# The 1/rms row of a norm, spread over the partitions by a trip through DRAM instead of by products with the identity

## The chip, the cores and the metric

The kernel runs on one core of a Trainium2 chip. What is measured is the device time of one execution in microseconds (us), as the median of several. Smaller is better.

A core has several engines that work side by side, each through its own list of instructions in order: TensorE (PE in the profile, with its weight loads as PEld), VectorE (DVE), ScalarE (ACT), GpSimd (POOL) and SyncE (SP), which in this kernel issues the transfers between DRAM and the on-chip memory SBUF. Where one needs what another makes, it waits on a semaphore, and everything queued behind it on that engine waits too.

## What is computed

A small decoder trunk on x of 1024 tokens by 1024 features: two layers, each a mixer and a SwiGLU feed-forward network (FFN), with a norm ahead of each and one at the end. Cut to what matters here:

```python
def rmsnorm(x, g):
    y = x * lax.rsqrt(jnp.mean(x * x, axis=-1, keepdims=True) + RMS_EPS)
    return y * g

def swiglu(h, w_gate, w_up, w_down):
    return (jax.nn.silu(h @ w_gate) * (h @ w_up)) @ w_down

def reference(x, ...):
    h = x
    for layer in range(2):
        hn = rmsnorm(h, mix_norm_g[layer])
        h = h + (even_mixer(hn, ...) if layer % 2 == 0 else odd_mixer(hn, ...))
        h = h + swiglu(rmsnorm(h, ffn_norm_g[layer]), ...)
    return rmsnorm(h, final_norm_g)
```

The even mixer holds a pooling mixer and a state-space scan (SSD), the odd one an RWKV-7 scan and a gated recurrence; each has an input and an output projection.

## The kernel before

**Layout.** Activations lie transposed in SBUF: features on the 128 partitions, tokens along the free axis. The 1024 tokens are worked on in two halves (hf 0 and 1) of H = 512; one tile is 128 features by 512 tokens, and eight tiles make a half. All large products run on TensorE in a split form: each operand is a high part and a low part, and three products (L370, L371, L372 in `dense`) make one. The weights come in blocks of 512 KB (`wload`, L323, issued on SP, three buffers `raw`), and are split by ACT (`whi`, L348) and DVE (`wlo`, L349) before TensorE uses them.

**Order.** `trunk` writes the stages of both halves one behind the other and weaves the scans in as side work: mixer and FFN of layer 0, half 0; output projection and then FFN of half 1, and so on. The order of instructions on each engine is not that of the text: the program is built under a context that schedules by a simulated time line, so a change in one place can move instructions around it.

**The norms.** `Stat.add` squares and sums the eight tiles of a half to one tile `nacc` (a token's sum is still spread over the partitions). `Stat.rstd` (L264 to L280) finishes it:

- L269: four products of TensorE with a column of ones sum `nacc` over the partitions. The result `ps_st` has 128 partitions by 4 columns: token c*128+p stands on partition p in column c.
- L272 and `rsqrt` (L206 to L215): twelve small DVE instructions on the tile `nst` make y = 1/rms in that form. The last of them is always an L215.
- L276: y is needed as a row r, along the free axis and the same on all partitions. Four products (y broadcast along the free axis, times the 128x128 identity) make it in `ps_rb`, eight PE instructions in the trace since a float32 product takes two passes.
- L279: ACT copies `ps_rb` to the SBUF tile `nrb` (128 by 512, two buffers). That is r.

`rstd` runs six times, mostly by `later(2, ...)`, that is two steps of `dense` behind the end of the sums. The numbers 1 to 6 are used below:

1. behind the output projection of half 0 in layer 0; r is used by the gate and up step of the FFN (DVE at L495, POOL at L498), whose input goes unscaled into the product (`gain_apply`), while the SSD of half 1 runs as side work;
2. behind that FFN; r is used by `norm_apply` (L300 on POOL, L304 on DVE) for the odd mixer of half 0;
3. behind the output projection of half 1; used by `norm_apply` for the FFN of half 1;
4. behind the FFN of half 1; used by `norm_apply` inside the output projection of half 0 in layer 1. Here the tiles are loaded back from DRAM (`hraw`, L285);
5. behind that output projection; used by `norm_apply` for the FFN of half 0 in layer 1;
6. behind the output projection of half 1 in layer 1; used by `stras_norm` (DVE at L598), which prepares the input of the last FFN. That FFN is computed by Strassen's scheme (products `py` at L663 and on, weights split by DVE and ACT); meanwhile the last steps of half 0's FFN run, with its final norm (`xo`, L583).

Elsewhere the kernel already spreads small values over the partitions through DRAM: the SSD's running sums (`cumT` to `cumd` at L901, loaded with a broadcast at L984) and the RWKV's norm of k (L1231 and L1262). The RWKV also copies a tile X to DRAM as `xd` in short runs and reads it back (L1352).

Of the kernel before, what the change touches and what calls it, by code (L numbers as in the profile page):

```python
# [5 lines left out]
F32 = mybir.dt.float32  # L6
# [7 lines left out]
P = 128  # L14
D = 1024
S = 1024
H = 512
# [69 lines left out]
class Trunk:  # L87
# [16 lines left out]
    def setup(self):  # L104
        nc, i = self.nc, self.i
        cst = self.cp.tile([P, NCONST], F32, name="cst")
        nc.gpsimd.dma_start(cst[:, :P], i["const"][:, :P])
        nc.gpsimd.dma_start(cst[:, P:], i["const"][:, P:NCONST])
        for n, (o, w) in CONST_COLS.items():
            if o < NCONST:  # L110
                setattr(self, "c_" + n, cst[:, o:o + w])
        self.ones = self.cp.tile([P, P], F32, name="ones")
        nc.gpsimd.memset(self.ones, 1.0)
        self.q = []


    def later(self, n, fn):
# [131 lines left out]
    class Stat:  # L249
# [15 lines left out]
        def rstd(self):  # L265
            tr, nc = self.tr, self.tr.nc
            ps = tr.psum("ps_st")
            for c in range(4):
                nc.tensor.matmul(ps[:, c:c + 1], self.acc[:, c * P:(c + 1) * P], tr.ones[:, :1], start=c == 0, stop=c == 3)  # L269
            st = tr.dp.tile([P, 3, 4], F32, name="nst", tag="nst", bufs=2)  # L270
            x, y, t = st[:, 0, :], st[:, 1, :], st[:, 2, :]
            nc.vector.tensor_scalar(x, ps[:, :4], 1.0 / D, EPS, op0=MULT, op1=ADD)  # L272
            tr.rsqrt(y, x, t)
            ps2 = tr.psum("ps_rb")
            for c in range(4):
                nc.tensor.matmul(ps2[:, c * P:(c + 1) * P], y[:, c:c + 1].to_broadcast([P, P]), tr.c_ident,  # L276
                                 start=True, stop=True)
            r = tr.dp.tile([P, H], F32, name="nrb", tag="nrb", bufs=2)
            nc.scalar.copy(r, ps2)  # L279
            return r  # L280

    def hload(self, hf, k):
# [1293 lines left out]
def trunk(tc, ins, out):  # L1576
    with ExitStack() as stack:
# [11 lines left out]
        with tc.tile_pool(name="ep", bufs=1) as ep:  # L1589
            t.setup()  # L1590
            hn, blk = t.start(ep, "xbc", 10)
            t.setup_params()
            t.even_open(ep)
            sA, sB = {}, {}
            side = Side(t.ssd(0, sA))
            m = t.in0(0, hn, sA, blk)
            weave(m, side, RATES["ssd0"], 10)
            xt = t.load_x(1, ep, "xbc", 10)
            hn = []
            hand(m, 8, t.norm_x(hn, xt), side, RATES["ssd0"])  # L1600
            t.zsync = side.finish
            weave(t.in0(1, hn, sB), side, RATES["ssd0"])
            side.finish()
            t.flush()
            side = Side(t.ssd(1, sB))
            hA, hn = [], []
            g = t.gain_apply(hn, hA, "ffn_norm_g", 0)
            st = hand(t.outproj(0, 0, wo0, t.yd[0], hA), 8, g, side, RATES["o0"], (4, 2))
            run_all(g)
            R["A"] = st.rstd()  # L1610
            side.step(RATES["b0"])
            st = weave(t.ffn(0, 0, hA, hn, None, lambda: R["A"]), side, RATES["ssd1"])
            side.finish()
            t.later(2, lambda: rstd("A", st))
            hB, hn = [], []
            stB = hand(t.outproj(1, 0, wo0, t.yd[1], hB), 8,
                       t.norm_apply(hn, None, lambda: R["A"], "mix_norm_g", 8, 0))
            t.flush()
        t.later(2, lambda: rstd("B", stB))
        with tc.tile_pool(name="op", bufs=1) as op, ExitStack() as late:  # L1620
            t.odd_open(op, late.enter_context(tc.tile_pool(name="oq", bufs=1)))
# [4 lines left out]
            st = weave(t.ffn(1, 0, hB, hn2), side, RATES["rw"])  # L1626
            side.finish()
            t.later(2, lambda: rstd("B", st))
            hA = []
            m = t.outproj(0, 1, wo1, t.yd[0], hA, t.hn2)  # L1630
# [51 lines left out]
```

## Time and profile before

| what | us |
|---|---|
| median of 3 runs (lowest to highest) | 2426.74 (2424.93 to 2427.56) |
| the profiled execution | 2427.69 |
| its span, first to last instruction | 2425.9 |
| TensorE busy | 2373.9 |
| VectorE busy | 1656.8 |
| ScalarE busy | 966.5 |
| GpSimd busy | 244.0 |

The mean clock that TensorE was granted is 0.992 of full speed. The profile's page gives the busy time of each engine and the chain of work that ended last, followed back from the last instruction. A time line lists single instructions or short groups: start, length, engine, line, operation, output and inputs with their shapes, and in brackets how long the engine was idle before and whose end released it. A row with "x8" is eight instructions in a row. All times count from the start of the span.

### The profile page before, as it was taken

What the parts mean: (1) busy time and instruction counts of PE and PEld (TensorE: products, weight loads), DVE (VectorE), ACT (ScalarE), POOL (GpSimd) and SP (SyncE); (2) the same over time, 40 slices, a digit from 0 to 9 for tenths busy, and PEclk for the clock granted to TensorE, in tenths of its full rate; (3) what the DMA queues carried; (4) which work ended last, traced back from release to release, by engine and by line L of the source; (5) the groups of instructions that cost most, each with busy time, mean ns of one, the idle gap of its engine ahead of it and who ended that gap; (6) DMA issues with size and microseconds to landing.
All of it is one profiled execution on the core that took longest, in us unless ns stands there. A gap on an engine that the chain in (4) does not pass through costs nothing.

```text
span 2425.9 us, 34902 instructions
## 1 busy us (share of the span) xinstructions
PE 2373.9 (98%) x13115; PEld 1986.4 (82%) x13115; DVE 1656.8 (68%) x3248; ACT 966.5 (40%) x1708; POOL 244.0 (10%) x231
## 2 busy tenths in 40 slices
PE   7989999999999999999999999999999999899998
PEld 6878887888878887788888888877888887899997
DVE  7878767764476675775565668676656548887775
ACT  4444433322234555233333346442333334454442
POOL 2131121211112010100000111010000000000000
PEclk9999999999999999999999999999999999899999
DMA  5433533333245333644324443335433442333332
GB/s 165 120 91 103 158 112 103 89 111 98 83 135 178 88 117 88 167 132 123 99 78 141 145 133 94 109 114 158 136 103 91 117 140 83 122 113 105 103 103 73
DMA packets 318874, 280.28 MB, mean 116 GB/s; under 512 B 46067, under 2 KB 296073, under 8 KB 318705
## 3 DMA queue, kind: packets, MB, share of 16 engines
q1 hardware_dynamic: 317872, 277.64, 39.0%
q8 instruction: 103, 1.69, 0.3%
q0 software_dynamic: 832, 0.41, 0.1%
q14 instruction: 67, 0.54, 0.1%
HBM read 247.51 MB, written 30.49 MB: 115 GB/s over the span
## 4 chain that ended last, share of the span: by engine, by line
PE 91%; DVE 4%; DMA 2%; issue 1%; SPq 1%; ACT 1%; POOL 0%; DVEq 0%; ACTq 0%; POOLq 0%
PE py L370 6%; PE py L371 6%; PE py L372 6%; PE pg L371 5%; PE pg L372 5%; PE pg L370 5%; PE pu L370 5%; PE pu L371 5%; PE pu L372 5%; PE pi L370 4%; PE pi L371 4%; PE pi L372 4%; PE po L370 2%; PE po L371 2%; PE po L372 2%; PE py L663 2%
## 5 line engine op out<-in xcount | busy, mean ns | idle before, releaser
L348 ACT CAST whi<-raw 128x512 fp32r<-128x512 f32 (+1 forms) x664 | 407.6, 619 | 877.8 <-PE pu L371 207.9
L349 DVE TENSOR_TENSOR wlo<-raw,whi 128x512 fp32r<-128x512 f32 (+1 forms) x664 | 477.6, 723 | 401.5 <-ACT whi L348 394.7
L371 PE MATMUL py<-actl,whi 128*128 128x512 f32 x672 | 266.8, 397 | 0.0
L370 PE MATMUL py<-acth,whi 128*128 128x512 f32 x672 | 264.0, 401 | 1.4 <-DVE sg L510 0.5
L372 PE MATMUL py<-acth,wlo 128*128 128x512 f32 x672 | 264.9, 395 | 0.0
L370 PE MATMUL pu<-hnh,whi 128*128 128x512 f32 x560 | 223.5, 400 | 0.0
L371 PE MATMUL pu<-hnl,whi 128*128 128x512 f32 x560 | 223.1, 398 | 0.0
L372 PE MATMUL pu<-hnh,wlo 128*128 128x512 f32 x560 | 222.2, 397 | 0.0
L370 PE MATMUL pg<-hnh,whi 128*128 128x512 f32 x528 | 211.2, 400 | 0.0
L371 PE MATMUL pg<-hnl,whi 128*128 128x512 f32 x528 | 209.3, 396 | 0.0
L372 PE MATMUL pg<-hnh,wlo 128*128 128x512 f32 x528 | 208.4, 396 | 0.0
L370 PE MATMUL pi<-hnh,whi 128*128 128x512 f32 x512 | 204.4, 399 | 0.1
L371 PE MATMUL pi<-hnl,whi 128*128 128x512 f32 x512 | 203.2, 397 | 0.0
L372 PE MATMUL pi<-hnh,wlo 128*128 128x512 f32 x512 | 201.7, 396 | 0.0
L370 PEld LDWEIGHTS py<-acth,whi 128*128 128x128 f32 x672 | 126.9, 189 | 31.3 <-issue 1.5
L372 PEld LDWEIGHTS py<-acth,wlo 128*128 128x128 f32 x672 | 127.1, 189 | 29.1
L371 PEld LDWEIGHTS py<-actl,whi 128*128 128x128 f32 x672 | 127.1, 189 | 27.3 <-DVE actl L236 0.2
L522 DVE TENSOR_TENSOR h<-h,py 128x512 f32<-128x512 f32 x160 | 107.6, 682 | 34.9 <-PE py L372 33.8
L370 PEld LDWEIGHTS pu<-hnh,whi 128*128 128x128 f32 x560 | 105.3, 188 | 25.4 <-issue 2.2
L372 PEld LDWEIGHTS pu<-hnh,wlo 128*128 128x128 f32 x560 | 105.4, 188 | 24.4 <-issue 0.7
L371 PEld LDWEIGHTS pu<-hnl,whi 128*128 128x128 f32 x560 | 105.2, 188 | 24.4
L371 PEld LDWEIGHTS pg<-hnl,whi 128*128 128x128 f32 x528 | 99.3, 188 | 23.1
(499 smaller groups left out, 4862.9 us busy)
## 6 DMA issues: line engine op xcount, KB each, us to landing
raw<-in_ffn_w_gate SPq DMA_DIRECT2D x88, 512.0 KB
raw<-in_ffn_w_up SPq DMA_DIRECT2D x88, 512.0 KB
raw<-in_ffn_w_down SPq DMA_DIRECT2D x68, 512.0 KB
raw<-in_od_w_in SPq DMA_DIRECT2D x44, 512.0 KB
raw<-in_ev_w_in SPq DMA_DIRECT2D x36, 512.0 KB
raw<-in_ffn_w_down SPq DMA_DIRECT2D x40, 256.0 KB
yraw<-yd SPq DMA_DIRECT2D x32, 256.0 KB
raw<-in_ev_w_out SPq DMA_DIRECT2D x16, 512.0 KB
```

What stands on the lines that cost most here:

```text
L348: nc.scalar.copy(hi[:, :m, :width], raw[:, k:k + m, :width])
L349: nc.vector.tensor_tensor(lo[:, :m, :width], raw[:, k:k + m, :width], hi[:, :m, :width].bitcast(F32), op=SUB)
L370: nc.tensor.matmul(o, wh[:, a:b], xh, start=st, stop=False)
L371: nc.tensor.matmul(o, wh[:, a:b], xl, start=False, stop=False)
L372: nc.tensor.matmul(o, wl[:, a:b], xh, start=False, stop=en)
L522: nc.vector.tensor_tensor(h[f], h[f], pp[t], op=ADD)
L663: mm(o, ah[:, c], bh, start=first and k == 0, stop=False, skip_group_check=True)
```

## The change

In `rstd` the four products and the ACT copy go. Instead y is stored to a row of 512 floats in DRAM, each time a new one (`nrow1` to `nrow6`), and that row is loaded with a broadcast to the 128 partitions of `nrb`. Both transfers are issued on SP, and the second waits until the first has landed. y has partition p and column c for token c*128+p, so the store writes 512 single floats: neighbours in the row come from neighbouring partitions.

```diff
@@ -112,6 +112,7 @@
         self.q = []
+        self.nstat = 0
@@ -271,12 +272,11 @@
             tr.rsqrt(y, x, t)
-            ps2 = tr.psum("ps_rb")
-            for c in range(4):
-                nc.tensor.matmul(ps2[:, c * P:(c + 1) * P], y[:, c:c + 1].to_broadcast([P, P]), tr.c_ident,
-                                 start=True, stop=True)
+            tr.nstat += 1
+            row = tr.dr.tile([1, H], F32, name=f"nrow{tr.nstat}")
+            nc.sync.dma_start(row.rearrange("o (c p) -> p (o c)", p=P), y)
             r = tr.dp.tile([P, H], F32, name="nrb", tag="nrb", bufs=2)
-            nc.scalar.copy(r, ps2)
+            nc.sync.dma_start(r, row.broadcast_to([P, H]))
             return r
```

The lines of the changed kernel between L115 and L279 stand one further down than before: the last step of y is L216 there, the store L277 and the load L279. TensorE's list is shorter by the six ps_rb, ACT's by six copies, and SP's is longer by twelve transfers. Around them the scheduler orders some rows anew.

On DVE at norm 1, the end of y (`nst`), the weights' low parts, the SSD (`dec`, `state`, `xdt`, `xd`, `yo`) and the gate step (`sg`) stand before in this order:

```order
L215 SCALAR_TENSOR_TENSOR nst<-nst 128x4
L349 TENSOR_TENSOR wlo<-raw,whi 128x2x256 x2
L1013 TENSOR_TENSOR dec<-dec,ps_cb 128x768
L495 TENSOR_TENSOR sg<-pg,nrb 128x512 x2
L1023 TENSOR_TENSOR state_3511<-state_3511,ps_st_3509 128x384
L993 TENSOR_TENSOR xdt<-xb,sm 128x384
L497 SCALAR_TENSOR_TENSOR sg<-th,sg 128x512 x2
L349 TENSOR_TENSOR wlo<-raw,whi 128x2x256
L1050 TENSOR_TENSOR yo<-ps_yT,par 128x384
L1032 TENSOR_TENSOR xd<-ps_yo,sm 128x384
```

Now, with the last L216 of y again as the first row:

```order
L216 SCALAR_TENSOR_TENSOR nst<-nst 128x4
L349 TENSOR_TENSOR wlo<-raw,whi 128x2x256
L495 TENSOR_TENSOR sg<-pg,nrb 128x512 x2
L349 TENSOR_TENSOR wlo<-raw,whi 128x2x256
L1050 TENSOR_TENSOR yo<-ps_yT,par 128x384
L497 SCALAR_TENSOR_TENSOR sg<-th,sg 128x512 x2
L1032 TENSOR_TENSOR xd<-ps_yo,sm 128x384
L1013 TENSOR_TENSOR dec<-dec,ps_cb 128x768
```

L1013, L1023 and L993 of the chunk in hand have moved ahead of y's last steps (they stand among the first steps on `nst` now), and with them the products that feed them on TensorE, which stand right behind the sum of `nacc`. L495 follows y with one wlo between, and behind it wait a wlo, L1050 and L1032.

On SP at the same place, the loads of weights with the stores of the SSD, before:

```order
L323 DMA raw<-in_ffn_w_gate 128x4x256 x2
L323 DMA raw<-in_ffn_w_up 128x4x256 x2
L1053 DMA yd_70<-yo 128x3x128
L984 DMA dec<-cumd_2650 128x6x128
L323 DMA raw<-in_ffn_w_down 128x4x256 x3
```

And now:

```order
L323 DMA raw<-in_ffn_w_gate 128x4x256 x2
L277 DMA nrow_3499<-nst 128x4x1
L279 DMA nrb<-nrow_3499 128x512
L323 DMA raw<-in_ffn_w_up 128x4x256
L984 DMA dec<-cumd_2650 128x6x128
L1053 DMA yd_70<-yo 128x3x128
L323 DMA raw<-in_ffn_w_up 128x4x256
```

The store and the load stand ahead of the two blocks of w_up, which SP issues only when the load of r has gone out.

On DVE at norm 6, the end of y, the weights' low parts, the last gate steps of half 0 (L501) and the first use of r (L598), before:

```order
L215 SCALAR_TENSOR_TENSOR nst<-nst 128x4
L349 TENSOR_TENSOR wlo<-raw,whi 128x2x256 x2
L501 SCALAR_TENSOR_TENSOR sg<-th,pg 128x512
L598 SCALAR_TENSOR_TENSOR hn<-hB,par,nrb 128x512 x2
L349 TENSOR_TENSOR wlo<-raw,whi 128x2x256
L610 TENSOR_TENSOR ts<-hn 128x256
L501 SCALAR_TENSOR_TENSOR sg<-th,pg 128x512
```

And now:

```order
L216 SCALAR_TENSOR_TENSOR nst<-nst 128x4
L349 TENSOR_TENSOR wlo<-raw,whi 128x2x256 x2
L598 SCALAR_TENSOR_TENSOR hn<-hB,par,nrb 128x512
L501 SCALAR_TENSOR_TENSOR sg<-th,pg 128x512
L349 TENSOR_TENSOR wlo<-raw,whi 128x2x256
L610 TENSOR_TENSOR ts<-hn 128x256
L501 SCALAR_TENSOR_TENSOR sg<-th,pg 128x512
```

One L598 has moved ahead of L501. On SP one load of w_down stands between the store and the load of r there.

## The prediction

> **What bounds the kernel now.** I read the page first (busy time by engine, shares of the chain), then the chain of waits for the places that the change touches, then the tables by stretch and the timelines there.
>
> ```profile
> span 2425.9 us, 34902 instructions
> PE 2373.9 (98%) x13115; PEld 1986.4 (82%) x13115; DVE 1656.8 (68%) x3248; ACT 966.5 (40%) x1708; POOL 244.0 (10%) x231
> PE 91%; DVE 4%; DMA 2%; issue 1%; SPq 1%; ACT 1%; POOL 0%; DVEq 0%; ACTq 0%; POOLq 0%
> ```
>
> TensorE is busy for 98% of the span, and 91% of the chain lies on it: nearly everywhere, a microsecond of matmul less is a microsecond less. All six spreading products (ps_rb) stand on the chain, each with the time it adds there in the second column:
>
> ```profile
> 349.59 0.89 PE ps_rb L276 x8
> 750.20 0.89 PE ps_rb L276 x8
> 800.48 0.89 PE ps_rb L276 x8
> 1390.07 0.89 PE ps_rb L276 x8
> 1437.78 0.89 PE ps_rb L276 x8
> 2018.95 0.89 PE ps_rb L276 x8
> ```
>
> One stretch is different, the one behind the sixth norm. In the timeline the columns are start, length, engine, line and operation, and in brackets the idle time before and what ended it:
>
> ```profile
> 2020.50 1.41 DVE L598 SCALAR_TENSOR_TENSOR hn<-hB,par,nrb 128x512 f32<-128x512 f32 x2 [0.20 <-ACT nrb L279]
> ...
> 2067.53 1.41 DVE L583 SCALAR_TENSOR_TENSOR xo<-pf,fst,grep 128x512 f32<-128x512 f32 x2
> ...
> 2068.68 0.55 PE L663 MATMUL py<-hnh,wah 128*128 128x256 f32 x1 [10.96 <-DVE xo L583]
> ```
>
> There TensorE stands still for 10.96 us until DVE has written xo. DVE works almost without a gap from its first use of the sixth row r (2020.50) up to that xo. So what counts there is when DVE can start L598 and not how soon TensorE is done.
>
> **What the change takes away.** Six groups of ps_rb at 0.89 us. Five (norms 1 to 5) lie where TensorE is the bound: 5 x 0.89 = 4.45 us less. The sixth is worth nothing by itself, since the DVE chain sets the restart. The six ACT copies of r go too; ACT is busy for 40% of the span and nothing but r's readers waited for them, so they are worth nothing beyond the arrival of r.
>
> **What it adds: a round trip through DRAM.** From y on DVE to r in SBUF stand now a store of 512 single floats and a broadcast load of 256 KB, one behind the other. The trace has no store of single floats. Its nearest rows: the 24 KB store of cumd, whose reader was issued 1.6 us later (59.68 to 61.29); the broadcast load behind it, on which DVE waited until 66.50, 5.2 us after its issue, for 384 KB; a plain 256 KB load issued at 1392.40 and used at 1395.12, 2.7 us; and, in the table of waits (sum, count, longest), the copy of 512 KB in runs of 128 bytes, 4096 packets, that held SP for up to 7.4 us.
>
> ```profile
> 59.68 0.39 SPq L901 DMA_DIRECT2D cumd<-cumT  x1
> 61.29 0.38 SPq L984 DMA_DIRECT2D dec<-cumd  x1
> 66.50 1.66 DVE L1001 SCALAR_TENSOR_TENSOR dec<-dec,sm,cst 128x128 f32<-128x128 f32 x6 [2.76 <-DMA dec<-cumd]
> ...
> 1392.40 2.90 SPq L285 DMA_DIRECT2D hraw<-hd  x3
> 1395.12 1.59 POOL L300 TENSOR_TENSOR hn<-hraw,nrb 128x512 f32<-128x512 f32 x1 [10.51 <-DMA hraw<-hd]
> ...
> SPq L1352 <- DMA xd<-X: 13.5, 2, 7.4
> ...
> q1 hardware_dynamic: 317872, 277.64, 39.0%
> ```
>
> A packet takes on average 0.390 x 16 x 2425.9 / 317872 = 0.048 us of one DMA engine. 512 single floats are 512 packets, 32 for each of 16 engines: up to 32 x 0.048 = 1.5 us. So the store is 1.6 to 7.4 us, and I take 1.6 + 1.5 = 3.1, as it is nearest to the small store. The load is 2.7 to 5.2 us; I take 2.7, the row of equal size. Round trip: **5.8 us**, bounds 4.3 and 12.6. The Trainium skill ("DMA: Bandwidth & Descriptors", Rules for kernel authors) speaks against the store's form: a strided last dimension is lowered to one descriptor per element. No row here shows what 512 of them cost; that rule gives no price, and the sum doesn't rest on it.
>
> **The same trip at each norm.** Norms 2, 3 and 5: their ps_rb, which reads y, starts at 750.20, 800.48 and 1437.78 in the chain above, so y is there by then, and DVE's first use of r comes at 768.5, 828.9 and 1463.9 in the groups of L304 (first and last start of a group stand behind the shortest, median and longest of its instructions). That is 18, 28 and 26 us of cover at the least, so the trip costs nothing there, even at 12.6.
>
> ```profile
> L304 DVE SCALAR_TENSOR_TENSOR hn<-hraw,par,nrb x8: 739/752/1781, 768.5 to 1403.3; 128x512 f32<-128x512 f32 x8
> L304 DVE SCALAR_TENSOR_TENSOR hn<-h,par,nrb x8: 739/745/752, 828.9 to 1545.3; 128x512 f32<-128x512 f32 x8
> ...
> L304 DVE SCALAR_TENSOR_TENSOR hn<-h,par,nrb x3: 744/749/752, 1463.9 to 1541.1; 128x512 f32<-128x512 f32 x3
> ```
>
> Norm 4 (y 1385.81, r read 1391.62): 5.8 us of trip end where r is read today, so DVE waits no longer; the last hnl is written at 1409.7 and the first product with this input starts at 1416.27, 6.5 us later at the least. A longer trip up to 12.3 us is hidden by that, unless DVE, which stands at L304 for r, fails to write wlo in time for the products now running. I put that at zero, and at 0.5 us with a slow store.
>
> ```profile
> 1385.65 0.16 DVE L215 SCALAR_TENSOR_TENSOR nst<-nst 128x4 f32<-128x4 f32 x1
> 1391.62 0.75 DVE L304 SCALAR_TENSOR_TENSOR hn<-hraw,par,nrb 128x512 f32<-128x512 f32 x1 [2.68 <-ACT nrb L279]
> ...
> 1407.95 1.78 DVE L302 SCALAR_TENSOR_TENSOR hnl<-hn,par,hnh 128x512 fp32r<-128x512 f32 x1
> 1416.27 0.40 PE L370 MATMUL pi<-hnh,whi 128*128 128x512 f32 x1
> ```
>
> Norm 1. The scheduler also puts L1013, L1023 and L993 of the SSD ahead of y now. By the starts of the rows that follow them they take 0.87 + 0.46 + 0.47 = 1.8 us, so y comes at 346.2 + 1.8 = 348.0 and r at 353.8.
>
> ```profile
> 346.03 0.16 DVE L215 SCALAR_TENSOR_TENSOR nst<-nst 128x4 f32<-128x4 f32 x1
> ...
> 350.75 0.95 DVE L1013 TENSOR_TENSOR dec<-dec,ps_cb 128x768 f32<-128x768 f32 x1 [0.88 <-PE ps_cb L1012]
> 351.62 1.28 DVE L495 TENSOR_TENSOR sg<-pg,nrb 128x512 f32<-128x512 f32 x2
> 352.82 0.55 DVE L1023 TENSOR_TENSOR state<-state,ps_st 128x384 f32<-128x384 f32 x1
> 353.28 0.55 DVE L993 TENSOR_TENSOR xdt<-xb,sm 128x384 f32<-128x384 f32 x1
> 353.75 1.92 DVE L497 SCALAR_TENSOR_TENSOR sg<-th,sg 128x512 f32<-128x512 f32 x2
> ...
> 359.93 0.81 PE L1017 MATMUL ps_st<-xd,xb 128*128 128x384 f32 x2
> ...
> 360.00:745.00 385.00, 383.50 (x1720) 310.56 (x1719) 240.29 (x423) 121.62 (x216) 58.99 (x46) 1.00 0.38 111
> ```
>
> Behind L495, which waits for r, DVE has a wlo and L1050 (yo) queued; for yo's input buffer TensorE waits with its next state product (L1017), which stands at 359.93 before. It comes sooner now by ps_rb and by eight products that moved behind it. In the stretch that follows TensorE does 1720 products in 383.5 us (first pair of numbers in the row), 0.22 us each, so it comes 0.89 + 1.8 sooner, at 357.2. L495, wlo and L1050 take 1.28 + 0.7 + 0.5 = 2.5 us, so r must be there by 354.7. With r at 353.8 the price is zero, with 0.9 us to spare; beyond that each microsecond of trip costs one.
>
> Norm 6. DVE is free of its wlo before the pair at 2018.0 and waited 1.61 us for th and 0.20 for r: the same start of L598 needs r by 2018.0 + 1.8 = 2019.8 in the new order, in which one L598 stands ahead of L501. y is there at 2014.3, so r comes at 2020.1: **0.3 us later**. A short trip gives back at most 0.7 + 0.2 = 0.9 us (one L598 in the gap before L501, and the last wait).
>
> ```profile
> 2014.15 0.16 DVE L215 SCALAR_TENSOR_TENSOR nst<-nst 128x4 f32<-128x4 f32 x1
> 2017.32 0.69 DVE L349 TENSOR_TENSOR wlo<-raw,whi 128x512 fp32r<-128x512 f32 x1 [2.08 <-ACT whi L348]
> 2019.62 0.69 DVE L501 SCALAR_TENSOR_TENSOR sg<-th,pg 128x512 f32<-128x512 f32 x1 [1.61 <-ACT th L500]
> ```
>
> SP's queue. Each second DMA waits for the first to land, so the weight loads behind it are held by some 3 us at six places. The lead of the weights hides that: in the whole run TensorE waited for a split weight once, for 4.3 us, though ACT had to wait for some loads itself.
>
> ```profile
> PE po L370 <- ACT whi L348: 4.3, 1, 4.3
> ACT whi L348 <- DMA raw<-in_ev_w_out: 23.6, 6, 6.6
> ```
>
> **The sum**, against the profiled execution's 2427.69 us: -4.45 + 0.3 = -4.15, so 2423.5. The median of the runs stands 0.95 us below that execution, so I forecast **2422.6 us** for the median. 0.2% of 2426.74 is 4.85 us, about what a measurement of this kernel can tell from no change; the bounds are 2421.9 and 2431.6, and the forecast lies just inside "same".
>
> **The rivals.** A, *a short trip*: store 1.6, load 2.7, so r of norm 6 comes at 2018.6 and the full 0.9 us comes back: -4.45 - 0.9 = -5.35, 2421.4 us. For it: the small store of cumd took 1.6 with 12 times the bytes. Against it: that one is in long runs. By the Trainium skill ("DMA: Bandwidth & Descriptors", Anatomy of one DMA) a DMA has some 2.0 us fixed, and the rest goes with its bytes; the trip would be estimated at 4.6 us, and this rival's time would follow.
>
> B, *the store of single floats is slow*, and DVE stands in front of r: with 7.4 + 2.7 = 10.1 us r comes at 358.1 in norm 1, 3.4 us late for TensorE, and at 2024.4 in norm 6, 4.6 us late for DVE. With 0.5 for norm 4 the sum is -4.45 + 3.4 + 4.6 + 0.5 = +4.05, 2430.8; with the slow load as well (12.6) both places grow by 2.5 and it is 2435.8. It turns slower than before from a trip of 8.3 us on, where norm 1 costs 1.6 and norm 6 costs 2.8. For it: 512 tiny packets, on the queue that feeds the weights. Against it: the 7.4 us row moves 4096 packets, eight times as many.
>
> C, *SP's queue*: at norm 2 the loads of the output projection's weights, for which ACT already waited up to 6.6 us, start 3 us later, and TensorE waits for a whi by as much. -4.15 + 3 = -1.15: 2425.6. For it: it is the place with the least lead. Against it: only one wait of TensorE in the whole run.
>
> D, *nothing comes of it*: what TensorE saves is waited out at the next transfer, 2426.7. Against it: the chain stays on TensorE for hundreds of microseconds behind each of the five.
>
> **The numbers.** Forecast 0.48, A 0.24, B 0.13, C 0.08, D 0.07. The range takes in A less the 1.8 us by which the fastest run lies under the median, 2419.6, and at the other end C, D and the first half of B, 2430.0. Faster than 2421.9: most of A (0.17) and of the forecast's spread about a third (0.17); slower than 2431.6: the far half of B and a little for mishaps on SP (0.12).
>
> **What would show it.** Right: PE's busy time shorter by some 5.3 us; the trip from the last step on nst to the first use of nrb some 6 us in norms 1, 4 and 6; DVE at L495 without a wait for nrb that TensorE then waits for; the wait of TensorE for xo still about 11 us. Wrong: a wait of more than 3 us at L495 or L598 with nrb's DMA as releaser (B), new waits of TensorE for whi behind 750 (C), or a span that shortens by more than 6 us.

## The result and the profile after

| | before | changed |
|---|---|---|
| median of 5 runs, us | 2426.74 (2424.93 to 2428.66) | 2450.92 (2447.87 to 2453.95) |
| the profiled execution, us | 2427.69 | 2448.73 |
| its span, us | 2425.9 | 2447.0 |
| TensorE busy, us | 2373.9 | 2375.8 |

The ratio is 1.0096, with a 95% interval of 1.0085 to 1.0107: the kernel is some 24 us slower. The forecast was 2422.6, the range 2419.6 to 2430.0. (One execution of the kernel with runs of 16 bytes, further down, took 4021.36 us at a mean granted clock of 0.63; its median leaves that one out.) The page of the changed kernel, with the rows that answer to those of before:

```profile
span 2447.0 us, 34816 instructions
PE 2375.8 (97%) x13067; PEld 1983.8 (81%) x13067; DVE 1656.4 (68%) x3248; ACT 963.2 (39%) x1702; POOL 243.6 (10%) x231
PE 88%; DVE 5%; DMA 4%; issue 1%; ACT 1%; POOL 0%; SPq 0%; DVEq 0%; ACTq 0%; POOLq 0%
```

TensorE's share of the chain falls from 91% to 88%, and that of transfers rises from 2% to 4%. Which transfers these are, the chain of waits says; its columns are start, length, and the work or transfer that the chain ran through:

```profile
346.84 10.29 DMA nrow<-nst
357.15 4.47 DMA nrb<-nrow
...
1391.70 9.65 DMA nrow<-nst
1401.37 4.58 DMA nrb<-nrow
...
2025.11 10.18 DMA nrow<-nst
2035.31 4.27 DMA nrb<-nrow
```

Where ps_rb stood with 0.89 us each, the store now stands with some 10 us and the load with 4.4, at norms 1, 4 and 6. Norms 2, 3 and 5 are not on the chain. The table of waits says who stood there (sum, times, longest):

```profile
DVE sg L495 <- DMA nrb<-nrow: 14.2, 1, 14.2
DVE hn L304 <- DMA nrb<-nrow: 11.2, 1, 11.2
DVE hn L598 <- DMA nrb<-nrow: 10.8, 1, 10.8
...
PE py L663 <- DVE xo L583: 10.7, 1, 10.7
PE ps_st L1017 <- DVE yo L1050: 8.4, 1, 8.4
PE po L370 <- ACT whi L348: 6.6, 2, 3.4
PE py L370 <- DVE sg L510: 4.4, 1, 4.4
PE pu L372 <- DVE wlo L349: 2.4, 1, 2.4
```

The wait for xo was there before (11.0); the 8.4, the 4.4 and the 2.4 are new, and so is one of the two waits for whi.

To place the loss, the table below takes the start of the product that sums `nacc` at each norm (L269, now L270), TensorE's restart behind xo (L663) and the end of the span, in both time lines. Each difference less the one above is what the stretch in between lost.

| from the profile, us | before | changed | later | lost in the stretch up to here |
|---|---|---|---|---|
| sum of norm 1 | 340.16 | 338.52 | -1.6 | -1.6 |
| sum of norm 2 | 741.36 | 749.19 | 7.8 | **9.5** (holds norm 1) |
| sum of norm 3 | 790.19 | 797.62 | 7.4 | -0.4 |
| sum of norm 4 | 1381.09 | 1386.95 | 5.9 | -1.6 |
| sum of norm 5 | 1427.42 | 1439.83 | 12.4 | **6.5** (holds norm 4) |
| sum of norm 6 | 2010.02 | 2020.80 | 10.8 | -1.6 |
| restart behind xo | 2068.68 | 2088.72 | 20.0 | **9.3** (holds norm 6) |
| end | 2425.9 | 2447.0 | 21.1 | 1.1 |

The three stretches with norms 2, 3 and 5 became 0.4 to 1.6 us shorter. (The first row, ahead of every norm, differs by -2.4 to +1.1 us in the executions below, so single stretches are good to a microsecond or two.)

At norm 1, in DVE's time line and in TensorE's, one row of each:

```profile
361.64 1.29 DVE L495 TENSOR_TENSOR sg<-pg,nrb 128x512 f32<-128x512 f32 x2 [14.22 <-DMA nrb<-nrow]
...
364.15 1.62 PE L1017 MATMUL ps_st<-xd,xb 128*128 128x384 f32 x2 [8.39 <-DVE yo L1050]
```

y was stored at 346.84 and r read at 361.64, 14.8 us later. yo is queued behind L495, and TensorE waits 8.39 us for it.

At norm 4, the same of DVE, ACT and TensorE:

```profile
1405.97 0.75 DVE L304 SCALAR_TENSOR_TENSOR hn<-hraw,par,nrb 128x512 f32<-128x512 f32 x1 [11.17 <-DMA nrb<-nrow]
1406.76 0.62 ACT L236 CAST hnh<-hn 128x512 fp32r<-128x512 f32 x1 [12.68 <-DVE hn L304]
1407.28 1.13 ACT L348 CAST whi<-raw 128x512 fp32r<-128x512 f32 x2
1407.95 0.80 PE L370 MATMUL po<-yh,whi 128*128 128x512 f32 x1 [3.19 <-ACT whi L348]
```

Here the wait runs through three engines: DVE stands at L304 for r, ACT stands at the cast of hn for DVE, and the weights' high part is queued on ACT behind that cast. TensorE runs dry of weights that it needs for the product in hand, long before it needs hn.

What the transfers did meanwhile is in the table by stretch; the last two columns are the busy share of the core's 16 DMA engines and the GB/s that they moved:

```profile
1391.70:1393.50 1.80, 1.80 (x10) 1.44 (x9) 0.61 (x1) 0.05 (x1) 0.00 (x0) 1.00 0.30 57
1393.50:1401.40 7.90, 7.90 (x36) 6.37 (x35) 0.69 (x1) 0.57 (x1) 0.00 (x0) 1.00 0.00 0
```

From 1.8 us behind the store's issue until its landing the DMA engines are idle for 7.9 us. So the 512 floats leave quickly, as the prediction's sum of packets said, and the time goes by before the landing is reported.

And the waits have an aftermath, in the same table; the eighth number, the third from the right, is the clock that TensorE was granted:

```profile
356.00:364.15 8.15, 0.00 (x1) 0.03 (x1) 2.51 (x5) 1.74 (x3) 0.00 (x0) 0.75 0.71 132
364.15:368.00 3.85, 3.85 (x9) 2.65 (x10) 3.85 (x6) 0.00 (x0) 3.32 (x3) 0.50 0.32 78
368.00:372.00 4.00, 4.00 (x16) 3.29 (x15) 4.00 (x11) 1.68 (x4) 0.57 (x1) 0.71 0.08 10
...
1408.00:1412.00 4.00, 4.00 (x11) 3.09 (x12) 3.75 (x6) 1.58 (x3) 1.28 (x1) 0.58 0.48 129
...
2053.00:2057.00 4.00, 4.00 (x11) 3.17 (x12) 4.00 (x8) 1.71 (x3) 0.00 (x0) 0.57 0.22 66
```

TensorE comes back from the wait of norm 1 at half its clock, for 3.85 us and 4 x 0.29 / 0.5 = 2.3 us more: 3.1 us of work lost. Behind the waits of norm 4 (1408) and norm 6 (2053) it is 3.4 us at half clock each, 1.7 lost each; behind the 2.4 us wait of norm 6 it is the same again (the clock is 0.63 from 2044 to 2047). Summed over the whole span in windows of 1 us, the half clock costs 17.6 us of TensorE's work now and 11.5 before. These 6.1 us are most of the 7.2 by which TensorE's busy time is longer than it should be: 1.9 us more than before, although 5.3 us of products are gone.

### The profile page after: what moved, and what is told of

Its sections match the earlier page's. It is cut to its first block, busy times and chain, and to the rows that moved or that the text cites. A ratio compares the mean times of both kernels' runs of the same rounds, so it can differ in the third digit from the quotient of the medians.

```text
span 2447.0 us, 34816 instructions
## 1 busy us (share of the span) xinstructions
PE 2375.8 (97%) x13067; PEld 1983.8 (81%) x13067; DVE 1656.4 (68%) x3248; ACT 963.2 (39%) x1702; POOL 243.6 (10%) x231
## 2 busy tenths in 40 slices
DMA packets 322906, 281.87 MB, mean 115 GB/s; under 512 B 49331, under 2 KB 299337, under 8 KB 322737
## 4 chain that ended last, share of the span: by engine, by line
PE 88%; DVE 5%; DMA 4%; issue 1%; ACT 1%; POOL 0%; SPq 0%; DVEq 0%; ACTq 0%; POOLq 0%
PE py L370 6%; PE py L371 6%; PE py L372 6%; PE pu L371 5%; PE pu L370 5%; PE pg L371 5%; PE pg L370 5%; PE pu L372 5%; PE pg L372 5%; PE pi L370 5%; PE pi L371 5%; PE pi L372 5%; PE po L372 2%; PE po L370 2%; PE po L371 2%; PE py L665 1%
## 5 line engine op out<-in xcount | busy, mean ns | idle before, releaser
L370 PE MATMUL py<-acth,whi 128*128 128x512 f32 x672 | 264.3, 402 | 4.7 <-DVE sg L510 4.4
L372 PE MATMUL py<-acth,wlo 128*128 128x512 f32 x672 | 265.7, 396 | 0.0
L372 PE MATMUL pu<-hnh,wlo 128*128 128x512 f32 x560 | 223.6, 399 | 2.4 <-DVE wlo L349 2.4
L370 PE MATMUL pu<-hnh,whi 128*128 128x512 f32 x560 | 224.8, 402 | 0.0
L370 PE MATMUL pg<-hnh,whi 128*128 128x512 f32 x528 | 211.3, 400 | 0.0
L372 PE MATMUL pg<-hnh,wlo 128*128 128x512 f32 x528 | 208.4, 396 | 0.0
L370 PE MATMUL pi<-hnh,whi 128*128 128x512 f32 x512 | 204.4, 400 | 0.4 <-DVE ccar L783 0.3
L372 PE MATMUL pi<-hnh,wlo 128*128 128x512 f32 x512 | 201.7, 396 | 0.0
L370 PEld LDWEIGHTS py<-acth,whi 128*128 128x128 f32 x672 | 127.2, 189 | 34.3 <-issue 4.8
L372 PEld LDWEIGHTS py<-acth,wlo 128*128 128x128 f32 x672 | 127.4, 190 | 29.3
L372 PEld LDWEIGHTS pu<-hnh,wlo 128*128 128x128 f32 x560 | 106.1, 189 | 27.3 <-DVE wlo L349 2.8
L370 PEld LDWEIGHTS pu<-hnh,whi 128*128 128x128 f32 x560 | 106.0, 189 | 25.8 <-issue 2.5
```

What stands on the lines that cost most here:

```text
L370: nc.tensor.matmul(o, wh[:, a:b], xh, start=st, stop=False)
L372: nc.tensor.matmul(o, wl[:, a:b], xh, start=False, stop=en)
```

## The experiments

The theory after this result, L: the store of single floats lands only after some 10 us, and three of the six norms have readers that can't wait that long. Its rival S: SP, which stands still between the store and the load, holds up the loads of the weights. In all kernels below the norms are numbered as above; "P" is a norm with the products as before.

### The trip made, but not used

The products stay at all six norms, and beside them the same store and load are issued, to a tile that nobody reads.

```diff
+                nc.sync.dma_start(row.rearrange("o (c p) -> p (o c)", p=P), y)
+                d = self.dp.tile([P, H], F32, name="ndum", tag="ndum", bufs=1)
+                nc.sync.dma_start(d, row.broadcast_to([P, H]))
```

> r comes from the products as before; store and broadcast load are made as well, to a tile that nobody reads. If the loss is the wait for r (theory L), nothing is lost here: 2425 to 2429 us. If it is SP, held for 10 us between store and load so that weights come late (theory S), most of the 24 us shows: over 2440.

Measured: 2427.91 us, ratio 1.0011 (1.0002 to 1.0020), 2.7 us slower. So most of the 24 us is the wait for r. S is not nothing: in this run's profile the sum of norm 4 starts 0.5 us later than before and that of norm 5 4.5, so the hold-up shows at norm 4 alone, where the loads of hraw stand behind it on SP:

```profile
DVE hn L329 <- DMA hraw<-hd: 7.8, 2, 7.5
```

Before, the longest such wait of DVE in this window (1385 to 1432) was 1.6 us. With the unused trip TensorE waits for weights in this window, four times and 3.0 us in all; before it waited for none there.

### The trip at some norms only

One kernel has the trip at norms 2, 3 and 5, three others at one norm each; the other norms have products.

```diff
+MODES = ['P', 'D', 'D', 'P', 'D', 'P']
...
+            if mode == "P":
+                ps2 = tr.psum("ps_rb")
...
+                return r
```

> The trip through DRAM at norms 2, 3 and 5 only, products at 1, 4 and 6. Theory L: 18 us and more of cover hide a trip of 15 us, and three ps_rb of 0.89 go: 2426.7 - 2.7 = 2424.0. Theory S: half of the six places, some 12 us slower, 2439.

> The trip through DRAM at norm 1 only. Theory L, with the 14.8 us measured in the changed kernel from the store's issue to L495 and the prediction's own rule that TensorE loses what the trip has over 6.7 us: +8.1 - 0.89, so 7.2 us slower than before. If the loss were spread over all six places: 4.

> The trip at norm 4 only. The prediction gave it at most 0.5 us of loss, so -0.4 net; theory L2 (DVE stands at L304 for r, and the weights' low parts behind it come late for the products in hand) gives the waits that TensorE shows in the changed kernel there, 3.2 + 0.9 + 1.0 and what its clock and ACT add, 5 to 6.5 us slower net.

> The trip at norm 6 only. Theory L with a trip of 14.7 us and the prediction's rule (DVE's chain loses what the trip has over 5.5 us, and the products that go there give nothing back): 9.2 us slower than before.

| trip at | median, us | ratio to before | us |
|---|---|---|---|
| 2, 3, 5 | 2422.28 | 0.9988 (0.9980 to 0.9997) | -2.9 |
| 1 | 2435.18 | 1.0036 (1.0024 to 1.0049) | +8.7 |
| 4 | 2430.74 | 1.0024 (1.0014 to 1.0033) | +5.8 |
| 6 | 2435.01 | 1.0043 (1.0030 to 1.0056) | +10.4 |

The last column is the ratio times the median of before in that series (2425.26, then 2424.81). The four add up to 22.0, beside 23.3 for the changed kernel (0.0096 x 2426.74); the interval of each is 2 to 3 us to either side. At norms 2, 3 and 5 the store takes as long as elsewhere (8 to 10 us in the profile) and costs nothing, and the three groups of 0.89 us come back almost in full: 2.9 for 2.7. Norm 1 and norm 6 lose what the rule of the prediction gives for the long trip (7.2 and 9.2 expected, inside both intervals; with the 3.1 us of half clock norm 1 would come to 10.3, which its interval of 5.8 to 11.9 holds as well). Norm 4 loses some 6 us, which the prediction had not seen. In the run with norm 6 alone, the waits are these:

```profile
DVE hn L617 <- DMA nrb<-nrow: 9.6, 1, 9.6
PE py L389 <- DVE sg L529: 6.5, 2, 5.3
```

### What the landing depends on

The products give r everywhere; beside them each norm stores its y once in another form, and SP then loads one float of it. From the store's issue to the load's issue is the landing. This kernel and the second one with layouts were run once each, for their profiles. For instance, 64 bytes apart:

```diff
+            w = self.dr.tile([P, 4, 16], F32, name="nw64")
+            nc.sync.dma_start(w[:, :, 0], y)
+            nc.sync.dma_start(d, w[:1, 0, :1])
```

> r comes from the products as before; beside them each norm stores its y once to DRAM in another form, and SP then loads one float of it, so that the time from the store's issue to the load's issue is the landing. Theory 1 (the number of pieces sets it): 512 single floats side by side (norm 1) 9 to 10 us, 512 floats 64 bytes apart (norm 2) and 1 KB apart (norm 3) the same, 128 pieces of 16 bytes (norm 4) and 128 single floats (norm 6) some 3 us, 4 pieces of 512 bytes (norm 5) some 2 us. Theory 2 (neighbouring floats in one block of DRAM hinder each other): norm 1 9 to 10 us, norms 2 and 3 only 2 to 3 us, norm 4 and 6 between. Theory 3 (it is the way through SP's queue, behind weights): all six some 9 us.

SP's time line of this run, norms 1 to 6 in pairs:

```profile
344.59 0.37 SPq L306 DMA_DIRECT2D nrow<-nst  x1
354.13 0.25 SPq L307 DMA_DIRECT2D ndum<-nrow  x1
...
746.05 0.57 SPq L310 DMA_DIRECT2D nw<-nst  x1
748.97 0.27 SPq L311 DMA_DIRECT2D ndum<-nw  x1
...
793.24 0.55 SPq L314 DMA_DIRECT2D nw1k<-nst  x1
795.43 0.26 SPq L315 DMA_DIRECT2D ndum<-nw1k  x1
...
1382.42 0.32 SPq L317 DMA_DIRECT2D nrow<-nst  x1
1383.82 0.25 SPq L318 DMA_DIRECT2D ndum<-nrow  x1
...
1436.02 0.28 SPq L324 DMA_DIRECT2D nrow<-nyr  x1
1437.27 0.25 SPq L325 DMA_DIRECT2D ndum<-nrow  x1
...
2010.43 0.34 SPq L327 DMA_DIRECT2D nrow<-nst  x1
2011.36 0.37 SPq L371 DMA_DIRECT2D raw<-in_ffn_w_down  x1
2017.83 0.26 SPq L328 DMA_DIRECT2D ndum<-nrow  x1
```

The same 512 floats take 9.5 us side by side, 2.9 us when they lie 64 bytes apart, and 2.2 us 1 KB apart. 128 pieces of 16 bytes take 1.4, four pieces of 512 bytes 1.25. So not the number of pieces sets it (theory 1 of that run falls), nor the way through SP's queue (theory 3): what is left is theory 2, that neighbouring floats hinder each other. 128 floats side by side took up to 7.4 us with a quarter of the pieces. A second run of layouts asked how near a neighbour must be:

> As the first run of layouts, r from the products. Landing of 128 floats side by side (norms 1 and 5), of 512 floats at 8 bytes (norm 2), 32 bytes (norm 3), 512 bytes (norm 4) and again 64 bytes (norm 6). If writes into one block of 64 bytes wait for each other: norms 1 and 5 some 7 us, norm 2 half the way of side by side (5 us), norm 3 (two to a block) 3 to 3.5, norms 4 and 6 2 to 3 us. If the block is 512 bytes: norm 3 still over 5 us, norm 6 some 3.

```profile
345.43 0.34 SPq L311 DMA_DIRECT2D nrow<-nst  x1
352.58 0.25 SPq L312 DMA_DIRECT2D ndum<-nrow  x1
...
746.53 0.37 SPq L308 DMA_DIRECT2D nw<-nst  x1
750.36 0.26 SPq L309 DMA_DIRECT2D ndum<-nw  x1
...
794.17 0.37 SPq L308 DMA_DIRECT2D nw<-nst  x1
796.07 0.25 SPq L309 DMA_DIRECT2D ndum<-nw  x1
...
2012.60 0.37 SPq L315 DMA_DIRECT2D nw<-nst  x1
2014.37 0.27 SPq L316 DMA_DIRECT2D ndum<-nw  x1
```

128 floats side by side: 7.2 us (and 7.1 at norm 5). 512 floats at 8 bytes: 3.8. At 32 bytes: 1.9, as quick as at 512 bytes (1.9). At 64 bytes, now in the order of the row, it is 1.8, so the 2.9 of the first run is no price of that distance. The time does not go with the distance alone, for the 16-byte pieces lie side by side too. It goes with the number of pieces that fall into the same 64 bytes: with 16 of them (floats side by side) it is 6.9 us and more over all runs, with eight (8 bytes apart) 3.8, with four (pieces of 16 bytes) 1.4 to 2.5, with two 1.9, with one 1.8 to 2.9. Whether the block is 32 or 64 bytes is open, for counted by 32 bytes the order is the same; 3 to 3.5 us were expected at 32 bytes if a block of 64 made a pair wait, and that did not come.

### Four runs instead of single floats

All six norms through DRAM; y is turned by one product to 4 partitions by 128 floats, copied by ACT, and stored in four pieces.

```diff
+                nc.tensor.transpose(ps2[:4, :P], y, tr.c_ident)
+                yr = tr.dp.tile([4, P], F32, name="nyr", tag="nyr", bufs=1)
+                nc.scalar.copy(yr, ps2[:4, :P])
+                nc.sync.dma_start(row.rearrange("o (c p) -> (o c) p", p=P), yr)
```

> All six norms through DRAM, but y is turned by one small product to 4 partitions by 128 floats and copied, so that the store has 4 pieces of 512 bytes. Theory L with a landing that goes with the pieces: some 2 us for the store, 4.4 for the load, 1 to 1.5 for turning, a trip of 8 us; norm 1 then costs some 1.5, norm 6 some 2.5, against 4.45 saved: 2425 to 2429. If the landing doesn't go with the form of the store: like the changed kernel, about 2451.

Measured: 2426.91 us, ratio 1.0005 (0.9996 to 1.0014), the time of before. The 24 us are gone with another form of the store. The waits for r are down to 3.3, 2.2 and 1.9 us:

```profile
DVE hn L617 <- DMA nrb<-nrow: 3.3, 1, 3.3
...
DVE sg L514 <- DMA nrb<-nrow: 2.2, 1, 2.2
DVE hn L323 <- DMA nrb<-nrow: 1.9, 1, 1.9
```

Up to the sum of norm 6 this run's profile is 7.3 us ahead of before (1.9 of them ahead of the first norm). It loses 2.8 up to the restart behind xo, where r is late for DVE, and another 2.8 in the last FFN, for which no single wait accounts. So the trip, even when short, didn't pay at norm 6 in this form.

### Runs of 16 bytes

The row is kept in the order in which y lies, so that each partition stores 16 bytes in one piece, and the readers of r take it with a stride of 4 floats.

```diff
-            nc.sync.dma_start(row.rearrange("o (c p) -> p (o c)", p=P), y)
+            nc.sync.dma_start(row.rearrange("o (p c) -> p (o c)", p=P), y)
...
-                    nc.vector.tensor_tensor(s, pg[t], r(), op=MULT)
+                    nc.vector.tensor_tensor(V4(s), V4(pg[t]), r(), op=MULT)
```

> All six norms through DRAM, the row in the order in which y lies (token c*128+p at place 4p+c), so that the store has 128 pieces of 16 bytes, which landed in 1.4 us in the first run of layouts; r is loaded in that order, and its readers take it with a stride of 4 floats. Theory L: a trip of 1.4 + 4.4 = 5.8 us, just the one that the prediction took, so its sum should come true: 2427 - 4.2, a ratio of 0.998, if the strided reading of r costs DVE and POOL nothing. If it costs them, a ratio of 0.999 to 1.002. If the loss had other causes than the landing: 1.005 and more.

Measured: 2434.54 us, ratio 1.0035 (1.0022 to 1.0049), which lies between the last two cases expected. The trip is nearly as short as meant (from the store's issue at 347.23 to L514 at 353.50 it is 6.3 us in norm 1), yet the kernel is 8.5 us slower. What is new is the price of reading r, in the groups of the tile nrb (shortest, median, longest, in ns):

```profile
L514 DVE TENSOR_TENSOR sg<-pg,nrb x22: 1052/1084/1120, 353.5 to 697.0; 128x512 f32<-128x512 f32 x22
L617 DVE SCALAR_TENSOR_TENSOR hn<-hB,par,nrb x8: 1121/1136/1149, 2021.8 to 2054.4; 128x512 f32<-128x512 f32 x8
```

The same groups before have medians of 691 and 744 ns: a stride of 16 bytes costs DVE 0.39 us on each of these instructions, 3.1 us on the eight L617 in the stretch where DVE sets the pace. In its profile the stretch with norm 6 loses 2.9 us and that with norm 1 2.6. Its profiled execution is only 5.0 us longer in span than before; the rest of the 8.5 is not placed. So this run doesn't show what the prediction's sum would be worth with a short trip; it shows another cost.

> As the one before, but with the products at norms 1 and 6. Theory L: four ps_rb go, nothing waits: -3.6 us, a ratio of 0.9985. If norms 1 and 6 lose nothing with the short trip either, it is no better than the run with all six.

Measured: 2423.65 us, ratio 0.9993 (0.9984 to 1.0002), no difference that can be told from before; the interval holds the 0.9985 expected too, so the run decides nothing there. It is better than the run with all six.

### The version that gains

> The changed kernel's store of single floats at norms 2, 3 and 5, the store of four runs at norm 4, products at 1 and 6. Theory L: three ps_rb and a fourth less the small product for turning y, 3.2 us less, a ratio of 0.9987; beside the run with norms 2, 3 and 5 alone it can't be told apart by more than 0.5 us.

Measured: 2422.96 us, ratio 0.9988 (0.9979 to 0.9997), as with norms 2, 3 and 5 alone. These two are faster than before by some 0.12%, with 1 just outside their intervals: the trip is worth its while exactly where the reader comes late.

## Why the prediction was wrong

**The bound.** Right: TensorE sets the pace nearly everywhere, and taking away three ps_rb where nothing waits gives 2.9 us, beside 3 x 0.89 = 2.7 counted.

**The store.** This is the step that failed. "So the store is 1.6 to 7.4 us, and I take 1.6 + 1.5 = 3.1, as it is nearest to the small store." It took 8.5 to 10.4 us, beyond the upper bound. The sum of packets was not the fault: the DMA engines were through in 1.8 us. The rows taken as nearest had long runs, or pieces of 128 bytes; none had neighbours written one float at a time, and the runs with layouts show that this is what costs. The Trainium skill ("DMA: Bandwidth & Descriptors", Rules for kernel authors) had warned of the form of this store, with one descriptor per element; the count of packets agrees (322906 against 318874, 672 more for each trip, 512 of them the floats). But the runs with layouts show that the count is not the price: 512 pieces 32 bytes apart land in 1.9 us. The same page (Specifications) says that under 512 bytes the transfer does a read-modify-write. The measurement narrows that: pieces of 16 bytes land in 1.4 us, floats 32 bytes apart in 1.9, and of the forms tried only those with eight or more pieces to 64 bytes take longer. That they do so because each write reads and rewrites the same block is a reading that fits, not one that these runs show.

**The load.** Taken as 2.7 us, measured 4.3 to 4.6, inside its bounds. It adds to the trip: 14.8 us at norm 1 where 5.8 was forecast and 12.6 was the upper end.

**Norms 2, 3 and 5.** Right: 18 us and more of cover hide a trip of 15.

**Norm 1.** The working was right and the trip was not: TensorE loses what the trip has over 6.7 us, 8.1 for 14.8, and it waited 8.4. What was left out is the 3.1 us that the half clock took behind it. (8.4 + 3.1 less the 0.89 of ps_rb is 10.6; the stretch as a whole lost 9.5.)

**Norm 6.** The same: what the trip has over 5.5 us, 9.0 for the 14.5 from y's end to L598, and the stretch lost 9.3. TensorE paid it not only at xo (whose wait stayed at 10.7) but ahead of it, at L372 and L370.

**Norm 4.** A second step that failed: "I put that at zero, and at 0.5 us with a slow store." It cost 6.5 in the changed kernel and 5.8 by itself. The prediction counted the cover of hn, which TensorE needs late, and not the queue of ACT: the cast of hn stands there ahead of the weights' high parts, and waits when DVE does. A part of it is also the hold-up of SP, up to 4 us by the run with the unused trip, where the same queues stood behind a late hraw in place of a late r. How much of the loss is either was not told apart; a trip issued by another engine than SP, which could tell, was not run.

**The clock.** No term of the sum had it. The Trainium skill ("TensorE: Matmul & The Clock Gate", Part 1) says that an array that was idle runs its first 3.4 us or so at half rate; the 3.4 us behind norms 4 and 6 agree, and at norm 1 it was 6.2. Where TensorE sets the pace, as at norms 1 and 4, such a wait of 3.2 or 8.4 us therefore costs 1.7 or 3.1 us more than its length; at norm 6 DVE sets the pace, and its 9.0 us are nearly the whole loss.

**SP's queue.** Rival C put it at norm 2; no loss shows there. It was at norm 4.

**The rivals.** B had the mechanism and the two main places, and gave 2430.8 to 2435.8. It was too low for three reasons: a store of 10 us instead of 7.4 (with a load of 4.3 to 4.6 that only its second figure covers), the 0.5 at norm 4, and the clock. The 4.6 us that A's paragraph estimates from a fixed cost and the bytes (the section cited there gives them for transfers that GpSimd issues, these go from SP) fit the trips with four runs, 4.4 to 5.5 us, and not those with single floats, 14.3 to 14.8.

## What to carry to other kernels

Price a small store by how many pieces it writes into the same few dozen bytes of DRAM, not by its bytes or the total of its pieces; turn the data on chip first, or leave it where the reader comes 15 us later. When an engine is to stand at a new wait, follow every queue that stands behind it, the next engine's too: at norm 4 the cover of the data itself was long enough, and the weights queued behind the cast were not covered. And where a trip's price is known only from unlike rows, the upper bound belongs well above the highest of them.

## What the runs showed of the hardware

- 512 single floats stored side by side from 128 partitions landed after 6.9 to 10.4 us in DRAM over all runs, 8 bytes apart after 3.8, 32 bytes apart after 1.9, 64 bytes apart after 1.8 and 2.9; 128 floats side by side after 7.1 to 7.4; 128 pieces of 16 bytes after 1.4 in the first run of layouts and up to 2.5 in use.
- The DMA engines had been idle for 7.9 us of the 9.7 of one such store.
- A broadcast load of a 2 KB row to 128 partitions took 3.2 to 5.4 us from its issue to the first reader that waited for it (4.3 to 4.6 in the changed kernel).
- Behind waits of 2.4 to 8.4 us TensorE's granted clock was 0.5 for 3.4 to 6.2 us of its work.
- A second operand read by DVE with a stride of 16 bytes made an instruction of 128x512 floats 0.39 us longer (1084 for 691 ns, 1136 for 744 ns).
